# A streaming encoder step: stick-breaking probabilities kept in PSUM, two gates moved to the SSM, the sample normed into its own operand

## The chip, the cores and the metric

The kernel runs on one core of a Trainium2 chip. The metric is device time in microseconds for one launch, the median of three runs.

## What is computed

One layer of a hybrid encoder over 1024 prompt tokens and, with the same weights, 64 sample tokens that also see 2048 cached keys and values. A normed input is projected to q, k, v (8 heads of 64), to the SSM's input u and to two sets of gates. Attention is stick-breaking, and an S5 state-space branch runs beside it; a gated merge, an output product, a SwiGLU feed-forward part and a gated embedding follow.

```python
def _sb_block(qb, start, k, v, q_offset):
    z = jnp.einsum('bqhd,bkhd->bhqk', qb, k) * (SB_HEAD_DIM ** -0.5)
    ...
    log_keep = jnp.where(visible, jax.nn.log_sigmoid(-z), 0.0)
    after = lax.cumsum(log_keep, axis=3, reverse=True) - log_keep
    w = jnp.where(visible, jnp.exp(jax.nn.log_sigmoid(z) + after), 0.0)
    return jnp.einsum('bhqk,bkhd->bqhd', w, v)
...
    merged = (jax.nn.sigmoid(g_attn) * (o_attn @ W['w_branch_attn'])
              + jax.nn.sigmoid(g_ssm) * (o_ssm @ W['w_branch_ssm']))
    x = x + _rmsnorm(merged @ W['w_out'], W['norm_mix_post'])
```

The kernel computes a row of w as sigmoid(z) times the product of sigmoid(-z) over all later keys: a multiplying scan from the right.

## The kernel before, in words

Products of fp32 precision are made of three passes (`mm3_iter`, lines 137 to 139) over a high and a low half of each operand; the halves of a weight unit are made by ScalarE (`wh`) and VectorE (`wl`) in `unit`. A projection unit of 128 output columns (`fm_iter`) is 8 steps x 3 passes x 3 chunks of tokens = 72 products. A **gate** is one such unit with a sigmoid behind it, stored to DRAM (`gates`, `columns`); there are 16. Two are made at the start. The other 14, and three columns of q, k, v for the first pair of heads, are one generator in `body`, `rest`. `fill(n)` takes n steps of it: they are the **fills**, TensorE work that is due late and placed where other work waits.

`rest` is drawn in this order: `fill(3 * G1)` after the SSM's scan (a step is a chunk there), then `ssm_out`, `fill(3 * G2)`, `glu`, and then attention.

*SSM.* `ssm_scan` runs on VectorE over `hist`. `ssm_out` copies the final states to `fs`, exchanges the halves of `hist` through transfers (`exchange`), transposes `fs` on TensorE for the output and then, per group, multiplies `ut` by `toep` and `hist` by `cm` (lines 577, 578), takes the gelu and stores the result for `glu`, which reads it back as `y` and splits it into `ya`.

*Attention.* `attention` projects pair 0 of the heads, then runs through the string `ORDER`, made by `order()`: a digit is a step of that head (four steps of two query blocks each), `d` a step of the sample's attention (five for each pair), `p` a third of a chunk of the next pair's projection, `g` a fill of the same size, `E` the early load of the merge's operands. `gs` says how many `g` fall into each pair of heads. The Tile framework then sets every engine's order from these; engines are in order and wait on semaphores.

A **stick** (`stick`) is one run of up to 512 keys for 128 queries: TensorE writes z to a PSUM bank of tag `z` (three banks); ScalarE makes p = sigmoid(-z) and w = sigmoid(z), both in SBUF; VectorE scans p in place from the right (line 735); GpSimd (for the first query block of a step, and for the sample) or VectorE (for the second) multiplies w by p shifted by one (line 737). Where a run continues one to its right, the last column is multiplied by the carried product on its own (line 739), and the new carried product is copied to a tile `cy` (line 742). Then w is transposed on TensorE into a `tr` bank (two banks), split into `wth` by ScalarE and `wtl` by VectorE, and multiplied by v into `av`. There are 116 sticks, 48 with a carried product.

`tok_out` transposes k and v of a pair for the outputs through tiles `ob`, two buffers.

*After attention.* `merge` makes the merged operand: prompt columns in `H`, the sample's in `HS` as high and low half. `mix_out` takes the sample first, then the prompt tiles, and writes the normed result with `pre` into `H`; `ffn_in` first copies the sample's part of `H` to `HD` (line 1214) and uses it in `decode_rows` (line 1182).

Of the kernel before, what the change touches and what calls it, by code (L numbers as in the profile page):

```python
# [8 lines left out]
F32 = mybir.dt.float32  # L9
# [8 lines left out]
SEQ = 1024  # L18
# [13 lines left out]
G1, G2 = 5, 4  # L32
# [33 lines left out]
ORDER = order(L=1.7, steps=(0, 0.23, 0.42, 0.76), d0=-0.09, d1=1.77, p0=-0.36, p1=1.49, gs=(9, 15, 3, 21), e=7)  # L66


class Net:
# [478 lines left out]
    def ssm_out(self, Q, U):  # L548
        nc = self.nc
        V, hist = nc.vector, self.hist  # L550

        ps = self.ps.tile([128, 512], F32, name="tr", tag="tr")
# [6 lines left out]
        for i in range(4):  # L559
            nc.tensor.transpose(ps[:16, i * 128:(i + 1) * 128], fs[:, i], self.ident)  # L560
        V.tensor_copy(fin, ps[:16].rearrange("g (i s) -> g i s", i=4))
        for i, o in enumerate((4, 5, 8, 9)):
            nc.sync.dma_start(self.O[o][0, 0].rearrange("(h g) p -> g h p", h=2),
                              fin[:, i].rearrange("g (h p) -> g h p", h=2))
# [3 lines left out]
        for b in range(2):  # L568
# [12 lines left out]
            for t in range(T):  # L581
                for h in range(2):
                    nc.sync.dma_start(dst[b, t, :, h], src[t * 16:(t + 1) * 16, h, b])

# [143 lines left out]
    def stick(self, P, z, n, carry, more, e):  # L728

        nc = self.nc  # L730
        w = P.tile([128, 512], F32, "w", "w")[:, :n]
        p = P.tile([128, 512], F32, "p", "p")[:, :n]
        nc.scalar.activation(p, z, AF.Sigmoid, scale=-1.0)  # L733
        nc.scalar.activation(w, z, AF.Sigmoid)
        nc.vector.tensor_tensor_scan(p[:, ::-1], p[:, ::-1], self.zero.to_broadcast([128, n]),  # L735
                                     1.0 if carry is None else carry, op0=OP.mult, op1=OP.add)
        (nc.gpsimd if e == 'g' else nc.vector).tensor_tensor(w[:, :n - 1], w[:, :n - 1], p[:, 1:], op=OP.mult)  # L737
        if carry is not None:
            nc.vector.tensor_tensor(w[:, n - 1:], w[:, n - 1:], carry, op=OP.mult)  # L739
        if more:  # L740
            carry = P.tile([128, 1], F32, "cy", "cy")
            nc.vector.tensor_copy(carry, p[:, 0:1])
        return w, carry
# [322 lines left out]
    def mix_out(self, P, U):  # L1066
# [5 lines left out]
        for t in (8, 0, 4, 1, 5, 2, 6, 3, 7):  # L1072
# [20 lines left out]
            self.pre(P, x, gp, *(self.H[:, :, i, c0:c0 + r] for i in range(2)), hook=hooks.get(t))  # L1093
# [115 lines left out]
    def ffn_in(self, PT, P):  # L1209
# [3 lines left out]
        HD = P.pool.tile([128, 8, 2 * DEC], F32R, name="HD")  # L1213
        A.activation(HD.rearrange("p k (i t) -> p k i t", i=2), self.H[:, :, :, SEQ:], AF.Copy)
# [262 lines left out]
def body(tc, I, O, dbg=None, upto=99):  # L1477
    with ExitStack() as ctx:
# [69 lines left out]
        PAA = pools(tc, "attA", dict(hl=2, qb0=1, qs0=2, raw=1, vs0=2, vn0=1, ob=2, kn0=1))  # L1548
        with pools(tc, "att", dict(qs1=2, vs1=2, vn1=1, kn1=1, qb1=1, ks=3, w=6, p=3, cy=6, wth=2, wtl=2,
                                   ot=1, o=1, od=1, kr=1, vc=1, kk=1, wtd=1), "right") as P:  # L1550
            N.ps.alias = {}
            N.attention(P, PAA, fill, early)
            with N.hold(1):
                fill(48)
# [6 lines left out]
        N.ps.alias = MAL  # L1561
        with pool("wout", "right") as PW:
            N.HS = PW.tile([128, 8, 2 * DEC], F32R, name="HS")
# [8 lines left out]
        with pool("tok", "right") as PT, pools(tc, "ffn1", dict(raw=2, dh=1, dl=1, st=3, s=4, g11=1, g12=1, g21=1, g22=1, u11=1, u21=1,  # L1572
                                                                  u22=1, q=1, y0=1, y1=1, yo=1)) as P:
            N.ps.alias = WAL
            N.ffn_in(PT, P)
        PA = ctx.enter_context(pools(tc, "acc", dict(ss=4, xr=1, xn=2, hT0=1, hT1=1)))
# [35 lines left out]
```

## Time and profile before

| | |
|---|---|
| median of three runs | 1753.33 us (1753.03 to 1759.03) |
| the profiled execution's own time | 1759.74 us |
| its span | 1758.0 us |
| TensorE (PE) busy | 1693.2 us, 96% |
| VectorE (DVE) busy | 1036.4 us, 59% |
| ScalarE (ACT) busy | 729.7 us, 42% |
| GpSimd (POOL) busy | 520.9 us, 30% |
| mean granted TensorE clock | 0.984 |

The profile is that of one execution. Busy times of an engine are unions of its instructions' spans; products on TensorE are pipelined, so the duration of one is about twice the distance at which they follow each other. An idle time is put down to the instruction whose end released the engine. [...]

### The profile page before, as it was taken

To read this page: it belongs to the slowest core of one execution; us is meant where nothing else is said; L and a number is where in the kernel's file an instruction comes from. 1 tells how busy PE (TensorE), PEld (TensorE's weight loads), DVE (VectorE), ACT (ScalarE), POOL (GpSimd) and SP (SyncE) were. 2 spreads that over 40 slices of the span, in tenths; PEclk is the share of its full clock that TensorE was granted. 3 is DMA by queue.
4 is the path that set the end of the run, shared out by engine and by line. 5 is a ranking of instruction groups with operands and counts; after the bars stand their busy time and mean duration, and the time that the engine had idled before them with its cause. 6 is when DMAs were issued, how large, how long until landed. Compare 5 with 4: busy or idle time off the path is not lost.

```text
span 1758.0 us, 24713 instructions
## 1 busy us (share of the span) xinstructions
PE 1693.2 (96%) x9092; PEld 1479.8 (84%) x9092; DVE 1036.4 (59%) x1579; ACT 729.7 (42%) x1355; POOL 520.9 (30%) x450
## 2 busy tenths in 40 slices
PE   8999999999999898899999999999999999999998
PEld 6999998988898877798787888888888877888886
DVE  7437916337777767767464655555555456445674
ACT  6431135125555555633344433333333344444542
POOL 2026200012323223224231544445444212001453
PEclk9999999999999989999999999999999999999999
DMA  8362563884444343147445544446444386655332
GB/s 286 92 153 64 126 137 110 249 213 102 105 102 107 70 109 89 56 151 236 144 157 184 164 140 139 146 133 199 140 140 148 109 302 206 205 189 169 106 110 89
DMA packets 220713, 258.23 MB, mean 147 GB/s; under 512 B 26144, under 2 KB 168592, under 8 KB 220576
## 3 DMA queue, kind: packets, MB, share of 16 engines
q1 hardware_dynamic: 219936, 255.20, 48.0%
q0 software_dynamic: 656, 1.44, 0.6%
q8 instruction: 72, 1.18, 0.3%
q14 instruction: 49, 0.40, 0.1%
HBM read 165.32 MB, written 76.51 MB: 138 GB/s over the span
## 4 chain that ended last, share of the span: by engine, by line
PE 75%; DVE 12%; DMA 5%; ACT 3%; issue 3%; POOL 1%; SPq 1%; DVEq 0%; POOLq 0%; ACTq 0%
PE pj L1206 14%; PE tr L1206 8%; PE pj L137 6%; PE pj L139 6%; PE pj L138 6%; PE z L1372 3%; PE z L1206 3%; DVE p L735 3%; PE pj L1372 3%; PE tr L1372 2%; PE av L811 2%; PE z L138 2%; PE z L139 2%; PE z L137 2%; PE tr L781 1%
## 5 line engine op out<-in xcount | busy, mean ns | idle before, releaser
L137 PE MATMUL pj<-H,wh 128*128 128x362 f32 (+3 forms) x648 | 218.4, 337 | 5.9 <-DVE ql L634 3.6
L139 PE MATMUL pj<-H,wl 128*128 128x362 f32 (+3 forms) x648 | 215.8, 334 | 0.6 <-DVE wl L115 0.6
L138 PE MATMUL pj<-H,wh 128*128 128x362 f32 (+3 forms) x648 | 215.4, 333 | 0.0
L126 DVE TENSOR_TENSOR wl<-raw,wh 128x1024 fp32r<-128x1024 f32 x96 | 136.2, 1422 | 113.0 <-ACT wh L125 109.8
L737 POOL TENSOR_TENSOR w<-w,p 128x383 f32<-128x383 f32 (+4 forms) x68 | 92.7, 1373 | 315.2 <-DVE w L739 187.6
L125 ACT ACTIVATE wh<-raw 128x1024 fp32r<-128x1024 f32 x96 | 101.1, 1058 | 112.7 <-PE z L1372 44.4
L137 PEld LDWEIGHTS pj<-H,wh 128*128 128x128 f32 x648 | 123.3, 190 | 7.6 <-DVE ql L634 3.9
L139 PEld LDWEIGHTS pj<-H,wl 128*128 128x128 f32 x648 | 123.1, 190 | 1.5 <-DVE wl L115 1.0
L138 PEld LDWEIGHTS pj<-H,wh 128*128 128x128 f32 x648 | 123.3, 190 | 0.9 <-issue 0.4
L1206 PE MATMUL pj<-H,s 128*128 128x512 f32 x480 | 118.2, 395 | 0.0
L148 POOL TENSOR_TENSOR rs<-rs,mhalf 128x1 f32<-128x1 f32 (+1 forms) x54 | 32.6, 606 | 279.2 <-DVE rs L147 279.1
L1206 PEld LDWEIGHTS pj<-H,s 128*128 128x128 f32 x480 | 89.9, 188 | 20.9 <-DVE c L1239 0.3
L125 ACT ACTIVATE s<-st 128x512 fp32r<-128x512 f32 x80 | 50.3, 629 | 127.6 <-PE pj L1206 116.8
L1140 POOL TENSOR_TENSOR st<-raw 128x512 f32<-128x512 f32 x40 | 61.3, 1532 | 126.4 <-issue 52.3
L126 DVE TENSOR_TENSOR s<-st,s 128x512 fp32r<-128x512 f32 x80 | 64.4, 805 | 41.5 <-ACT s L125 40.9
L119 ACT ACTIVATE wh<-raw 128x1024 fp32r<-128x1024 f32 (+1 forms) x52 | 46.6, 898 | 98.9 <-PE av L138 51.4
L115 DVE TENSOR_TENSOR wl<-raw,wh 128x1024 fp32r<-128x1024 f32 (+1 forms) x50 | 51.0, 1021 | 57.9 <-ACT wh L119 57.8
L785 ACT ACTIVATE wth<-tr 128x512 fp32r<-128x512 f32 (+2 forms) x112 | 50.3, 453 | 83.3 <-PE tr L781 42.8
L786 DVE TENSOR_TENSOR wtl<-tr,wth 128x512 fp32r<-128x512 f32 (+2 forms) x112 | 55.2, 496 | 49.4 <-ACT wth L785 48.9
L733 ACT ACTIVATE p<-z 128x512 f32<-128x512 f32 (+4 forms) x116 | 59.0, 509 | 42.6 <-PE z L835 16.7
L735 DVE TENSOR_TENSOR_SCAN p<-p,zero 128x384 f32<-128x384 f32 (+4 forms) x68 | 73.9, 1094 | 0.2
L1206 PE MATMUL pj<-H,wh 128*128 128x512 f32 x224 | 71.1, 394 | 0.6 <-ACT H L125 0.4
(553 smaller groups left out, 4626.8 us busy)
## 6 DMA issues: line engine op xcount, KB each, us to landing
sd<-c SPq DMA_DIRECT2D x77, 256.0 KB, 3.1
raw<-sd SPq DMA_DIRECT2D x77, 256.0 KB, 2.8
raw<-in_w_in_dram SPq DMA_DIRECT2D x32, 512.0 KB, 5.4
raw<-in_w_ffn_gate_dram SPq DMA_DIRECT2D x22, 512.0 KB, 3.7
raw<-in_w_ffn_up_dram SPq DMA_DIRECT2D x22, 512.0 KB, 4.8
wd<-in_w_ffn_down_dram SPq DMA_DIRECT2D x44, 256.0 KB, 3.4
td<-wd SPq DMA_DIRECT2D x22, 512.0 KB, 3.1
raw<-td SPq DMA_DIRECT2D x44, 256.0 KB, 3.0
```

The costliest lines, as they stand in the source:

```text
L125: self.nc.scalar.activation(wh, raw, AF.Copy)
L126: self.nc.vector.tensor_sub(wl, raw, wh)
L137: self.nc.tensor.matmul(out, wh, xh, start=i == 0, stop=False)
L138: self.nc.tensor.matmul(out, wh, xl, start=False, stop=False)
L139: self.nc.tensor.matmul(out, wl, xh, start=False, stop=i == n - 1)
L733: nc.scalar.activation(p, z, AF.Sigmoid, scale=-1.0)
L735: nc.vector.tensor_tensor_scan(p[:, ::-1], p[:, ::-1], self.zero.to_broadcast([128, n]), 1.0 if carry is None else carry, op0=OP.mult, op1 ...
L737: (nc.gpsimd if e == 'g' else nc.vector).tensor_tensor(w[:, :n - 1], w[:, :n - 1], p[:, 1:], op=OP.mult)
L786: nc.vector.tensor_sub(wl[:, a:b], ps[:, a:b], wh[:, a:b])
L1140: op(t, x, y)
L1206: self.nc.tensor.matmul(out, a[i][:, k], b[j][:, k], start=start and k == i == j == 0, stop=stop and k == 3 and i == 1, skip_group_check=n ...
L1372: nc.tensor.matmul(B[b + n], x[:, 0, c], y[:, 1], start=new and p == j == 0, stop=p == 10 and j == 2, skip_group_check=not new)
```

## The change

- `stick`: w is made first; sigmoid(-z) is written over z in its PSUM bank; the scan reads that bank and writes p, now a tile of 513 columns whose last column holds the carried product. One product then covers the carried column too. The carried product is copied into column 512 of the tile that the next run will use (`late`). Lines 739 and the tile `cy` are gone.
- `G1` 5 to 6, `G2` 4 to 5, `gs` (9, 15, 3, 21) to (9, 12, 3, 6): a gate more ahead of the SSM's output, one more behind it, 18 steps of `g` (two gates) fewer in attention.
- `ssm_out`: the states' transposes and their stores come behind the output products, in a `z` bank instead of a `tr` bank.
- `mix_out`, `ffn_in`: the sample is normed into `HS`, which lives on until the feed-forward part; the tile `HD` and its copy are gone.
- Buffers: `w` 6 to 5, `p` 3 to 5 (wider), `cy` gone, `ob` 2 to 1.

```diff
-G1, G2 = 5, 4
+G1, G2 = 6, 5
...
-ORDER = order(L=1.7, steps=(0, 0.23, 0.42, 0.76), d0=-0.09, d1=1.77, p0=-0.36, p1=1.49, gs=(9, 15, 3, 21), e=7)
+ORDER = order(L=1.7, steps=(0, 0.23, 0.42, 0.76), d0=-0.09, d1=1.77, p0=-0.36, p1=1.49, gs=(9, 12, 3, 6), e=7)
...
     def ssm_out(self, Q, U):
-        ps = self.ps.tile([128, 512], F32, name="tr", tag="tr")
         fin = Q.tile([16, 4, 128], F32, name="fin")
         fs = Q.tile([128, 4, 16], F32, name="fs")
...
         self.exchange(hist[:, :, :, :NCH], X)
-        for i in range(4):
-            nc.tensor.transpose(ps[:16, i * 128:(i + 1) * 128], fs[:, i], self.ident)
-        V.tensor_copy(fin, ps[:16].rearrange("g (i s) -> g i s", i=4))
-        for i, o in enumerate((4, 5, 8, 9)):
-            nc.sync.dma_start(self.O[o][0, 0].rearrange("(h g) p -> g h p", h=2),
-                              fin[:, i].rearrange("g (h p) -> g h p", h=2))
...
+        ps = self.ps.tile([128, 512], F32, name="z", tag="z")
+        for i in range(4):
+            nc.tensor.transpose(ps[:16, i * 128:(i + 1) * 128], fs[:, i], self.ident)
+        V.tensor_copy(fin, ps[:16].rearrange("g (i s) -> g i s", i=4))
...
-    def stick(self, P, z, n, carry, more, e):
+    def stick(self, P, z, n, late, more, e):
         w = P.tile([128, 512], F32, "w", "w")[:, :n]
-        p = P.tile([128, 512], F32, "p", "p")[:, :n]
-        nc.scalar.activation(p, z, AF.Sigmoid, scale=-1.0)
+        p = P.tile([128, 513], F32, "p", "p") if late is None else late
+        c = 512 - n
         nc.scalar.activation(w, z, AF.Sigmoid)
-        nc.vector.tensor_tensor_scan(p[:, ::-1], p[:, ::-1], self.zero.to_broadcast([128, n]),
-                                     1.0 if carry is None else carry, op0=OP.mult, op1=OP.add)
-        (nc.gpsimd if e == 'g' else nc.vector).tensor_tensor(w[:, :n - 1], w[:, :n - 1], p[:, 1:], op=OP.mult)
-        if carry is not None:
-            nc.vector.tensor_tensor(w[:, n - 1:], w[:, n - 1:], carry, op=OP.mult)
+        nc.scalar.activation(z, z, AF.Sigmoid, scale=-1.0)
+        nc.vector.tensor_tensor_scan(p[:, c:512][:, ::-1], z[:, ::-1], self.zero.to_broadcast([128, n]),
+                                     1.0 if late is None else p[:, 512:], op0=OP.mult, op1=OP.add)
+        m = n - (late is None)
+        (nc.gpsimd if e == 'g' else nc.vector).tensor_tensor(w[:, :m], w[:, :m], p[:, c + 1:c + 1 + m], op=OP.mult)
         if more:
-            carry = P.tile([128, 1], F32, "cy", "cy")
-            nc.vector.tensor_copy(carry, p[:, 0:1])
-        return w, carry
+            late = P.tile([128, 513], F32, "p", "p")
+            nc.vector.tensor_copy(late[:, 512:], p[:, c:c + 1])
+        return w, late
...
-            self.pre(P, x, gp, *(self.H[:, :, i, c0:c0 + r] for i in range(2)), hook=hooks.get(t))
+            out = (self.H[:, :, i, c0:c0 + r] for i in range(2)) if t < 8 else (self.HS[:, :, i * DEC:i * DEC + DEC] for i in range(2))
+            self.pre(P, x, gp, *out, hook=hooks.get(t))
...
-        HD = P.pool.tile([128, 8, 2 * DEC], F32R, name="HD")
-        A.activation(HD.rearrange("p k (i t) -> p k i t", i=2), self.H[:, :, :, SEQ:], AF.Copy)
+        HD = self.HS
...
-        PAA = pools(tc, "attA", dict(hl=2, qb0=1, qs0=2, raw=1, vs0=2, vn0=1, ob=2, kn0=1))
-        with pools(tc, "att", dict(qs1=2, vs1=2, vn1=1, kn1=1, qb1=1, ks=3, w=6, p=3, cy=6, wth=2, wtl=2,
+        PAA = pools(tc, "attA", dict(hl=2, qb0=1, qs0=2, raw=1, vs0=2, vn0=1, ob=1, kn0=1))
+        with pools(tc, "att", dict(qs1=2, vs1=2, vn1=1, kn1=1, qb1=1, ks=3, w=5, p=5, wth=2, wtl=2,
```

How the change moves instructions, as built. TensorE in the SSM, before: the second pair of the states' transposes stands amid the fills that run ahead of the first `z<-hist` (`av<-H` are products of a gate, `fs` the copied states).

```order
L139 MATMUL av<-H,wl 128x362
L137 MATMUL av<-H,wh 128x362
L138 MATMUL av<-H,wh 128x362
L560 MATMUL tr<-ident,fs 16x128 x2
L139 MATMUL av<-H,wl 128x362
L137 MATMUL av<-H,wh 128x362
L138 MATMUL av<-H,wh 128x362
```

The same engine now: all four stand amid the fills behind the last `z<-hist`.

```order
L139 MATMUL pj<-H,wl 128x362
L137 MATMUL av<-H,wh 128x362
L138 MATMUL av<-H,wh 128x362
L579 MATMUL z<-ident,fs 16x128 x4
L139 MATMUL av<-H,wl 128x362
L137 MATMUL av<-H,wh 128x362
L138 MATMUL av<-H,wh 128x362
```

From row 929, where a gate begins in both, to the first `z<-hist` there are 172 rows before and 171 now: 169 and 170 products of gates. Behind the last `z<-hist` 93 stood before the first product of `glu`; now it is 245.

VectorE in attention, the start of a step of the sample and the heads beside it, before (the scan is listed as SCALAR_TENSOR_TENSOR, of line 735; `ba` is the merge's early operand):

```order
L735 SCALAR_TENSOR_TENSOR p<-p,cy,zero 128x512
L739 TENSOR_TENSOR w<-w,cy 128x1
L735 SCALAR_TENSOR_TENSOR p<-p,zero 128x384
L742 COPY cy<-p 128x1
L735 SCALAR_TENSOR_TENSOR p<-p,zero 128x512
L742 COPY cy<-p 128x1
L798 TENSOR_TENSOR o<-av,ot 64x256
L737 TENSOR_TENSOR w<-w,p 128x511
```

And now, the same place (the scan is line 737, the product line 740, the copy line 743):

```order
L737 SCALAR_TENSOR_TENSOR p<-z,p,zero 128x512
L743 COPY p<-p 128x1
L737 SCALAR_TENSOR_TENSOR p<-z,zero 128x384
L743 COPY p<-p 128x1
L737 SCALAR_TENSOR_TENSOR p<-z,zero 128x512
L799 TENSOR_TENSOR o<-av,ot 64x256
L740 TENSOR_TENSOR w<-w,p 128x511
L743 COPY p<-p 128x1
```

The order of the steps stayed; the single-column products went out and the scans read z.

Fills between one product `z<-kk,qb` or `z<-kn,qb` and the next, in TensorE's order, for the twenty steps of the sample (the last counted to the merge):

| | |
|---|---|
| before | 119, 34, 96, 51, 12, 75, 72, 111, 57, 21, 57, 57, 72, 30, 24, 0, 33, 57, 30, 120 |
| now | 135, 18, 96, 51, 12, 75, 63, 105, 48, 21, 57, 57, 81, 21, 9, 0, 9, 15, 9, 102 |

## Rows read from the trace of the kernel before

**Rows 1.** The page, part 1: engine, busy us, share of the span, instructions.
```profile
PE 1693.2 (96%) x9092; PEld 1479.8 (84%) x9092; DVE 1036.4 (59%) x1579; ACT 729.7 (42%) x1355; POOL 520.9 (30%) x450
```

**Rows 2.** Timeline of PE: start us, us, engine line operation [idle before, releaser].
```profile
197.45 0.39 PE L560 MATMUL tr<-ident,fs 128*16 128x128 f32 x2 [1.52 <-DVE fs L555]
...
222.34 0.60 PE L560 MATMUL tr<-ident,fs 128*16 128x128 f32 x2 [3.18 <-DVE fs L556]
...
232.49 0.39 PE L578 MATMUL z<-hist,cm 128*128 128x137 f32 x2
...
250.80 0.28 PE L578 MATMUL z<-hist,cm 128*128 128x137 f32 x1
...
268.89 0.49 PE L137 MATMUL tr<-ya,wh 128*128 128x364 f32 x1 [2.38 <-ACT ya L125]
...
344.71 0.33 PE L139 MATMUL tr<-bs,wl 128*128 128x362 f32 x1
345.21 0.33 PE L139 MATMUL tr<-bs,wl 128*128 128x362 f32 x1
```

**Rows 3.** Windows: stretch, busy us (x) of PE, PEld, DVE, ACT, POOL, granted clock.
```profile
220.00:230.00 10.00, 7.66 (x32) 7.59 (x32) 5.08 (x24) 1.06 (x1) 0.00 (x0) 0.66 0.53 138
```

**Rows 4.** Windows of three seven-scan cycles of attention, columns as before.
```profile
431.10:453.50 22.40, 20.86 (x134) 18.04 (x132) 18.24 (x28) 13.28 (x28) 6.34 (x4) 1.00 0.41 97
671.80:695.30 23.50, 18.94 (x116) 16.33 (x115) 18.36 (x31) 13.20 (x29) 6.33 (x4) 0.93 0.25 72
695.30:714.70 19.40, 18.81 (x123) 17.16 (x124) 16.38 (x30) 13.14 (x30) 5.37 (x4) 1.00 0.35 111
```

**Rows 5.** Timeline of DVE, SP and ACT around the end of the SSM scan.
```profile
208.81 1.22 DVE L115 TENSOR_TENSOR wl<-raw,wh 128x1024 fp32r<-128x1024 f32 x1
...
224.98 0.63 SPq L543 DMA_DIRECT2D us<-hist  x1
...
230.12 1.11 ACT L545 COPY hist<-us 64x1096 f32<-64x1096 f32 x1 [0.70 <-DMA us<-hist]
```

**Rows 6.** Groups by line and form: count, busy us, mean ns, idle before.
```profile
L735 DVE TENSOR_TENSOR_SCAN p<-p,zero 128x512 f32<-128x512 f32 x24 | 40.6, 1691 | 0.1
L739 DVE TENSOR_TENSOR w<-w,cy 128x1 f32<-128x1 f32 x48 | 12.8, 267 | 0.0
L737 DVE TENSOR_TENSOR w<-w,p 128x511 f32<-128x511 f32 x32 | 28.2, 881 | 1.5
L737 POOL TENSOR_TENSOR w<-w,p 128x511 f32<-128x511 f32 x24 | 43.9, 1828 | 201.8 <-DVE w L739 170.5 <-PE pj L139 13.7 <-ACT p L733 12.1
L733 ACT ACTIVATE p<-z 128x512 f32<-128x512 f32 x56 | 34.2, 610 | 29.6 <-PE z L835 16.7 <-POOL w L737 6.3 <-PE av L811 4.1
```

**Rows 7.** Timeline of DVE, POOL and PE in the cycles before 696 and at 754.
```profile
665.84 0.69 DVE L786 TENSOR_TENSOR wtl<-tr,wth 128x512 fp32r<-128x512 f32 x1 [1.25 <-ACT wth L785]
...
666.24 1.60 POOL L715 TENSOR_TENSOR vs<-ob,vs 128x256 fp32r<-128x256 f32 x2
...
673.63 1.28 DVE L735 TENSOR_TENSOR_SCAN p<-p,cy,zero 128x512 f32<-128x512 f32 x1 [1.27 <-ACT p L733]
...
675.02 0.95 DVE L735 TENSOR_TENSOR_SCAN p<-p,zero 128x384 f32<-128x384 f32 x1
...
676.07 1.86 DVE L735 TENSOR_TENSOR_SCAN p<-p,zero 128x512 f32<-128x512 f32 x1
...
677.85 0.63 PE L764 MATMUL z<-ks,qs 128*128 128x512 f32 x2
...
682.92 0.67 DVE L737 TENSOR_TENSOR w<-w,p 128x511 f32<-128x511 f32 x1
...
753.70 1.09 POOL L737 TENSOR_TENSOR w<-w,p 128x511 f32<-128x511 f32 x1 [3.58 <-DVE w L739]
```

**Rows 8.** DMA issues, 360 to 700 us: count, KB each, median us to landing.
```profile
out_dram<-ob SPq DMA_DIRECT2D x15, 256.0 KB, 2.4
```

**Rows 9.** Waits of PE, 930 to 950 us: us, times, longest.
```profile
PE z L1182 <- ACT HD L1214: 1.7, 1, 1.7
```

More of the change, by code (lines that the diff above doesn't have):

```diff
@@ L583, in ssm_out @@
                     nc.sync.dma_start(dst[b, t, :, h], src[t * 16:(t + 1) * 16, h, b])
+        ps = self.ps.tile([128, 512], F32, name="z", tag="z")
+        for i in range(4):
+            nc.tensor.transpose(ps[:16, i * 128:(i + 1) * 128], fs[:, i], self.ident)
+        V.tensor_copy(fin, ps[:16].rearrange("g (i s) -> g i s", i=4))
+        for i, o in enumerate((4, 5, 8, 9)):
+            nc.sync.dma_start(self.O[o][0, 0].rearrange("(h g) p -> g h p", h=2),
+                              fin[:, i].rearrange("g (h p) -> g h p", h=2))
     def glu(self, P):
@@ L1561, in body @@
         N.ps.alias = MAL
+        hs = pool("hs", "right")
+        N.HS = hs.__enter__().tile([128, 8, 2 * DEC], F32R, name="HS")
         with pool("wout", "right") as PW:
-            N.HS = PW.tile([128, 8, 2 * DEC], F32R, name="HS")
             with pools(tc, "mrgB", dict(braw=1, ga=2, gs=2)) as P:
@@ L1575, in body @@
             N.ffn_in(PT, P)
+        hs.__exit__(None, None, None)
         PA = ctx.enter_context(pools(tc, "acc", dict(ss=4, xr=1, xn=2, hT0=1, hT1=1)))
```

## The prediction

> **What bounds the kernel now.** I read the page first: TensorE is busy 1693.2 us, 96% of the span of 1758.0 [rows 1], so all that any edit can win beside removed TensorE work is 65 us of idle time, and what a lowered clock costs. The profiled execution took 1759.74 us, 6.4 above the median of the runs, 1753.33; differences below are taken from the first and applied to the second. Next I asked the waits and the timeline of TensorE where it stands still. Two places concern the change.
>
> First, the SSM. Fills are issued about 0.167 us apart (the last two rows of [rows 2]: three products in 0.50 us). Amid them TensorE stands 1.52 and 3.18 us for the two transposes of `fs`, and 2.38 us at the first GLU product [rows 2]. [...]
>
> Second, attention. I cut it at the products `z<-kk,qb` of `decode`, one per step of the sample, into 20 cycles, and asked for busy times by cycle. Twelve cycles have seven scans. In eight of these the fill is 57 products or fewer and VectorE has 16 to 18.5 us to do: they start at 431.1, 531.5, 578.5, 628.0, 671.8, 695.3, 714.7 and 738.5 and last 179.5 us together [rows 4]. Here the number of fills hardly sets the length: by the built order the cycle at 671.8 has 33 and takes 23.5 us, the one at 431.1 has 51 and takes 22.4 [rows 4]. VectorE, and the chain through ScalarE, GpSimd and the two `tr` banks, sets it. In the other cycles TensorE is busy nearly throughout, and a fill costs its 0.167 us.
>
> **The change, part by part.**
>
> *Two gates into the SSM: +18.7 us there.* A gate is 72 products, two are 144, or 24.0 us at 0.167. How much falls into gaps? By the built order the first `z<-hist` still has 170 fills ahead of it after 195.9 us (169 now), but no `fs` transposes. So TensorE comes earlier, and what is late next is `hist`: the exchange's transfers are issued at 224.98 when the scan ends, and its copy on ScalarE is done at 230.12 + 1.11 = 231.2 [rows 5]. VectorE's order in the scan is the same, so the second unit's low half is still ready at 208.81 + 1.22 = 210.0 [rows 5], where TensorE, no longer held, would arrive at 208.3. From 210.0 the remaining 98 fills last until 226.4: it idles 4.8 us for `hist`. Then come 17.2 us in place of 18.5 (from 232.5 to 251.0 [rows 2]), with 18 fills in between where 26 were, and some 2.5 us for the lowered clock, from the stretch that fell to 0.66 [rows 3]: until 250.9. Then 245 fills and the four transposes, 41.5 us, which cover the GLU's wait for `ya` completely, then 432 GLU products at 0.166: 364.2 us. Now the last of them ends at 345.5 [rows 2]. So 24.0 us of work cost 18.7; the gap moves more than it closes. The bounds are 15 (`hist` and the second unit in time) and 24 (nothing covered).
>
> *Fill taken from attention: -6.5 us.* Counting fills between two `z<-kk,qb` in both orders, the 144 come off as follows: 105 in the eight VectorE-bound cycles (9, 9, 24, 42 and 21 in the second, fourth, fifth, sixth and seventh of them), which I price at nothing because VectorE's time covers them, and a net 39 where TensorE is the bound (+16, -16, -9, -6, +9, -15 and, behind the last scan, -18): 39 x 0.167 = 6.5. Were none covered it would be 24.0; that is the far bound.
>
> *The scan reads PSUM; the carried column goes: -16.8 us.* Per seven-scan cycle: three single-column products at 0.267 are gone, 0.8 [rows 6]. The scans of 512 with a constant start average 1.69 us [rows 6], but 1.28 is what a 512 scan takes with GpSimd quiet, against 1.86 while GpSimd multiplies [rows 7]. A VectorE product with one input in PSUM kept its 0.69 us beside GpSimd at work [rows 7]. I therefore take the scans at the quiet price: 24 x 0.41 plus a little for the others, 12 us over 116 scans, 0.7 to 0.9 a cycle. VectorE's own 511 product is lifted from 0.67 to a mean of 0.88 by the same collisions [rows 6, 7]; two a cycle, 0.4. A weight split now and then moves out with the gates, 0.3. GpSimd's product, 1.83 on average and 1.09 where nothing met it [rows 6, 7], ends earlier and releases transposes, 0.3 more. Against it: the scan now follows ScalarE's second sigmoid, not its first, and at the start of a cycle VectorE has nothing else: +0.61 [rows 6]. Net 2.1 us in eight cycles, 16.8. Bounds: nothing, if PSUM is no quieter and the later start costs its 0.6 four times a cycle; 27 if the shorter chain counts in all twelve long cycles (2.25 each).
>
> What a scan from PSUM costs by itself no row shows. VectorE's 512 difference from PSUM takes no longer than the 0.67 to 0.69 of one from SBUF [rows 7], so I add nothing; the bounds are 0 and the 0.41 that would undo the quiet price. [...]
>
> *One `ob` buffer instead of two: +2 us.* The second and third copies of K's transposes now wait for the transfer before them, 2.4 us to landing [rows 8], with VectorE's queue (`wtl` for the next products) behind them. Twice in each of three pairs would be 14 us of VectorE waiting. But in two of the three the built order has 18 or more fills on TensorE around them, 3 us each, so I take 2. Bounds 0 and 14.
>
> *The sample normed into `HS`: -1.7 us.* The copy to `HD` goes, and with it the 1.7 us for which TensorE waits for it [rows 9]. Nothing covers it now and nothing replaces it, as `HS` is complete long before. Removed SBUF pressure elsewhere (`w` 5 for 6, `p` 5 for 3) I cost at nothing: five tiles are one cycle's.
>
> **Sum:** 18.7 - 6.5 - 16.8 + 2 - 1.7 = -4.3 us: 1755.4 for the profiled execution, **1749** on the median. Half a per cent, 8.8 us, is about what a measurement of this kernel can tell from no change, so I forecast no change that can be told.
>
> **Rivals.**
> *A, the attention gains more.* All twelve long cycles shorten, by 2.25 us, `ob` costs nothing, and the second unit's low half is no obstacle (-1.7): 17.0 - 6.5 - 27 - 1.7 = -18, 1735. For it: GpSimd's products shrink from 1.83 towards 1.09 in every cycle, and the transposes and `wtl` follow them. Against it: the four cycles with over 57 fills have TensorE busy nearly all the time. Part of it, about 1740, is the more probable form.
>
> *B, slower: PSUM banks come free too late.* Three `z` banks serve the queue. Now a bank is free after the second sigmoid; then only after its scan, on VectorE, behind whatever stands there. In a long cycle four of seven `z` must wait for a scan three places back. A new `z` needs about 0.63 us on TensorE [rows 7], two sigmoids at 0.61 [rows 6] and some 0.15 of signalling: 2.0 us, while two scans, 0.95 for 384 and 1.28 for 512, last 2.2 [rows 7]. It decides against the change as soon as that chain grows by 0.3 us: then VectorE waits, TensorE stands in its order with transposes behind it. Two such waits of 0.7 us in twelve cycles are 17 us: 1766. For it: the fills that filled those waits are just the ones removed. Against it: in the built order `z` is spread between transposes. [...] No row here shows yet what holding a bank costs.
>
> *C, the scans stay as slow.* Should GpSimd hold VectorE up as before, only the removed columns (0.8) and the moved splits count, less the later start: 0.5 x 8 = 4, and the sum is +8.5, 1762. [...]
>
> **How the numbers follow.** Forecast 0.52, its own range 1742 to 1757; of it 0.13 falls below 1744.5 and 0.02 above 1762. A 0.25, nearly all faster (0.23). B 0.15, slower but for 0.02. C 0.08, on the border: 0.06 same, 0.02 slower. Faster 0.13 + 0.23 = 0.36; same 0.37 + 0.02 + 0.02 + 0.06 = 0.47; slower 0.02 + 0.13 + 0.02 = 0.17. The range for 8 in 10 runs from A's end to the middle of B: 1735 to 1763.
>
> **What would show it.** Right: TensorE waits near 226 us for `hist` and nowhere before the GLU, whose last product ends near 364; scans of 512 read 1.2 to 1.3 us in every place and GpSimd's 511 product close to 1.1; the eight long cycles fall by some 2 us each though their fill is gone; attention ends about 20 us after that with 144 fills fewer; no wait at the first L1182. Wrong: scans above 1.5 us (C); TensorE standing at `z<-ks,qs` until a scan (B); cycles shortened by the fills they lost (then VectorE was not the bound, and A or more holds).

## The result and the profile after

| | before | after |
|---|---|---|
| median | 1756.70 us (6 runs, 1753.03 to 1759.03) | 1770.26 us (6 runs, 1766.91 to 1772.89) |
| profiled execution, its own time | 1759.74 us | 1769.70 us |
| its span | 1758.0 us | 1767.6 us |

The ratio is 1.0079, with a 95% interval of 1.0064 to 1.0093: slower by 0.8%, outside the range of the prediction, which had seen no change as the likeliest. By the medians that is 13.6 us; the two profiled executions lie 10.0 us apart. The page of the changed kernel, part 1, answers to [rows 1]:

```profile
PE 1693.1 (96%) x9092; PEld 1473.7 (83%) x9092; DVE 1005.4 (57%) x1531; ACT 733.4 (41%) x1354; POOL 485.8 (27%) x450
```

TensorE is busy as long as before, VectorE 31 us and GpSimd 35 us less. So the 9.6 us by which the span grew are idle time on TensorE: 1767.6 - 1693.1 = 74.5 us against 1758.0 - 1693.2 = 64.8.

**The SSM went as forecast.** TensorE's timeline of the changed kernel, start and duration in us, answers to [rows 2]:

```profile
229.77 0.80 PE L570 MATMUL z<-hist,cm 128*128 128x137 f32 x2 [4.66 <-DVE hist L546]
...
249.74 0.40 PE L570 MATMUL z<-hist,cm 128*128 128x137 f32 x2
...
290.89 0.33 PE L137 MATMUL pj<-ya,wh 128*128 128x364 f32 x1
...
362.43 0.33 PE L139 MATMUL pj<-bs,wl 128*128 128x362 f32 x1
```

One wait of 4.66 us for `hist`, none for `ya`, and the GLU's last product ends at 362.8 instead of 345.5: 17.2 us later, for 24 us of work moved there.

**The scans became short too.** Groups by form in attention, changed kernel, columns as in [rows 6]:

```profile
L737 DVE TENSOR_TENSOR_SCAN p<-z,p,zero 128x512 f32<-128x512 f32 x32 | 40.5, 1275 | 28.4 <-ACT z L736 28.4
...
L740 POOL TENSOR_TENSOR w<-w,p 128x512 f32<-128x512 f32 x24 | 30.0, 1251 | 209.2 <-DVE p L737 209.2
L737 DVE TENSOR_TENSOR_SCAN p<-z,zero 128x512 f32<-128x512 f32 x24 | 29.3, 1220 | 2.5 <-ACT z L736 2.5
...
L740 DVE TENSOR_TENSOR w<-w,p 128x511 f32<-128x511 f32 x24 | 16.3, 679 | 0.1
```

1.22 us for 1.69, GpSimd's product 1.25 for 1.83, VectorE's 0.68 for 0.88 [rows 6].

**But attention gave back too little.** From the GLU's last product to the merge's first it lasts 413.1 us, 13.0 less than before, where the prediction's terms made 21.3. What VectorE waited for before its copies to `ob`, from 365 to 775 us, first in the kernel before and then in the changed one:

```profile
its engine sat idle before it (us, times) until:
  PE tr L705: 7.8, 7
  DMA out_dram<-ob: 3.6, 2
```

```profile
its engine sat idle before it (us, times) until:
  DMA out_dram<-ob: 19.9, 7
```

**And the merge grew by 5.2 us**, from 48.2 to 53.4 between its first and its last product. Two waits in TensorE's timeline there that the kernel before does not have, and ScalarE's timeline ahead of the first:

```profile
789.14 0.43 PE L137 MATMUL z<-ba,wh 128*128 128x364 f32 x1 [1.10 <-ACT wh L119]
...
821.86 0.43 PE L139 MATMUL pj<-ba,wl 128*128 128x364 f32 x1 [1.99 <-DVE wl L115]
```

```profile
785.84 0.51 ACT L125 ACTIVATE H<-ga 128x362 fp32r<-128x362 f32 x1 [0.80 <-POOL ga L946]
788.06 0.51 ACT L125 ACTIVATE H<-ga 128x364 fp32r<-128x364 f32 x1 [1.71 <-POOL ga L946]
788.47 1.14 ACT L119 ACTIVATE wh<-raw 128x512 fp32r<-128x512 f32 x2
```

The split of the next weights stands behind pieces of `H<-ga` that wait for GpSimd. In the kernel before it stands ahead of them:

```profile
780.99 0.63 ACT L119 ACTIVATE wh<-raw 128x512 fp32r<-128x512 f32 x1 [1.64 <-PE av L138]
781.53 0.49 ACT L125 ACTIVATE H<-ga 128x364 fp32r<-128x364 f32 x1
```

### The profile page after: what moved, and what is told of

Same layout as the page of the kernel before. It is cut to its first block, busy times and chain, and to the rows that moved or that the text cites. A ratio compares the mean times of both kernels' runs of the same rounds, so it can differ in the third digit from the quotient of the medians.

```text
span 1767.6 us, 24576 instructions
## 1 busy us (share of the span) xinstructions
PE 1693.1 (96%) x9092; PEld 1473.7 (83%) x9092; DVE 1005.4 (57%) x1531; ACT 733.4 (41%) x1354; POOL 485.8 (27%) x450
## 3 DMA queue, kind: packets, MB, share of 16 engines
q8 instruction: 71, 1.16, 0.3%
## 4 chain that ended last, share of the span: by engine, by line
PE 76%; DVE 11%; DMA 7%; ACT 3%; issue 2%; POOL 1%; SPq 1%; DVEq 0%; POOLq 0%; ACTq 0%
PE pj L1208 14%; PE tr L1208 7%; PE pj L137 7%; PE pj L139 6%; PE pj L138 6%; PE z L1373 3%; PE z L1208 3%; PE pj L1373 3%; DVE p L737 2%; PE z L138 2%; PE z L137 2%; PE z L139 2%; PE tr L1373 2%; PE av L1373 1%; PE z L765 1%
## 5 line engine op out<-in xcount | busy, mean ns | idle before, releaser
L137 PE MATMUL pj<-H,wh 128*128 128x362 f32 (+3 forms) x632 | 211.6, 335 | 5.5 <-DVE ql L634 2.8
L139 PE MATMUL pj<-H,wl 128*128 128x362 f32 (+3 forms) x632 | 209.0, 331 | 0.4 <-DVE wl L115 0.4
L138 PE MATMUL pj<-H,wh 128*128 128x362 f32 (+3 forms) x632 | 208.9, 331 | 0.0
L740 POOL TENSOR_TENSOR w<-w,p 128x383 f32<-128x383 f32 (+4 forms) x68 | 61.5, 908 | 328.4 <-DVE p L737 327.8
L137 PEld LDWEIGHTS pj<-H,wh 128*128 128x128 f32 x632 | 119.5, 189 | 7.7 <-DVE ql L634 2.9
L138 PEld LDWEIGHTS pj<-H,wh 128*128 128x128 f32 x632 | 119.1, 189 | 0.8 <-issue 0.4
L139 PEld LDWEIGHTS pj<-H,wl 128*128 128x128 f32 x632 | 119.0, 188 | 0.8 <-DVE wl L115 0.6
L1208 PEld LDWEIGHTS pj<-H,s 128*128 128x128 f32 x480 | 89.8, 188 | 20.9 <-DVE c L1240 0.3
L787 DVE TENSOR_TENSOR wtl<-tr,wth 128x128 fp32r<-128x128 f32 (+2 forms) x112 | 54.4, 494 | 47.1 <-ACT wth L786 46.7
L786 ACT ACTIVATE wth<-tr 128x128 fp32r<-128x128 f32 (+2 forms) x112 | 49.3, 448 | 69.7 <-PE tr L782 55.0
L735 ACT ACTIVATE w<-z 128x512 f32<-128x512 f32 (+4 forms) x116 | 57.8, 498 | 37.2 <-PE z L836 15.9
L737 DVE TENSOR_TENSOR_SCAN p<-z,p,zero 128x512 f32<-128x512 f32 (+1 forms) x48 | 52.0, 1094 | 28.4 <-ACT z L736 28.4
```

The costliest lines, as they stand in the source:

```text
L137: self.nc.tensor.matmul(out, wh, xh, start=i == 0, stop=False)
L138: self.nc.tensor.matmul(out, wh, xl, start=False, stop=False)
L139: self.nc.tensor.matmul(out, wl, xh, start=False, stop=i == n - 1)
L737: nc.vector.tensor_tensor_scan(p[:, c:512][:, ::-1], z[:, ::-1], self.zero.to_broadcast([128, n]), 1.0 if late is None else p[:, 512:], op ...
L740: (nc.gpsimd if e == 'g' else nc.vector).tensor_tensor(w[:, :m], w[:, :m], p[:, c + 1:c + 1 + m], op=OP.mult)
L787: nc.vector.tensor_sub(wl[:, a:b], ps[:, a:b], wh[:, a:b])
```

## The experiments

The stages of each profiled execution, from TensorE's timeline, in us: the end of the GLU's last product, from there to the first product of the merge (attention), and from that to the merge's last. "Profiled" is that execution's own time. Executions of one kernel scatter by some 4 us about their median, and the profiled ones lie on either side of it (e17's is 7 us above), so a single profile tells stages apart, and the medians tell the sum. Each run was measured beside runs of the kernel before, whose median was 1754.7 to 1756.8; "over before" is the difference from those, and the ratio is to them as well. Where two runs were not measured together, their difference is better read from this column than from the medians.

| run | GLU ends | attention | merge | profiled | median | over before | ratio to before, 95% |
|---|---|---|---|---|---|---|---|
| before | 345.5 | 426.1 | 48.2 | 1759.7 | 1756.7 | | |
| after | 362.8 | 413.1 | 53.4 | 1769.7 | 1770.3 | +13.6 | 1.0064 to 1.0093 |
| e1_old_fill | 344.6 | 424.8 | 53.5 | 1761.7 | 1763.7 | +8.4 | 1.0029 to 1.0063 |
| e2_gates_only | 360.8 | 420.8 | 48.7 | 1770.1 | 1773.5 | +18.2 | 1.0085 to 1.0121 |
| e3_ob2 | 363.0 | 409.3 | 53.4 | 1768.9 | 1764.6 | +9.3 | 1.0031 to 1.0068 |
| e4_HD_copy | 363.6 | 412.1 | 53.0 | 1767.7 | 1771.4 | +16.1 | 1.0067 to 1.0110 |
| e5_scan_sbuf | 362.2 | 431.7 | 53.9 | 1792.0 | 1786.4 | +29.6 | 1.0147 to 1.0190 |
| e6_scan_psum_only | 363.0 | 405.2 | 48.1 | 1760.9 | 1758.2 | +1.4 | 0.9988 to 1.0012 |
| e7_psum_old_fill | 343.9 | 418.7 | 48.1 | 1752.4 | 1753.0 | -3.8 | 0.9972 to 0.9992 |
| e8_column_old_fill | 344.5 | 426.6 | 48.1 | 1759.2 | 1762.9 | +6.1 | 1.0023 to 1.0046 |
| e9_merge_order | 364.2 | 418.6 | 48.1 | 1773.8 | 1773.5 | +18.5 | 1.0093 to 1.0122 |
| e10_ob1 | 364.2 | 408.0 | 48.1 | 1762.6 | 1766.3 | +11.2 | 1.0050 to 1.0076 |
| e11_pool_products | 346.7 | 412.2 | 48.3 | 1750.1 | 1750.1 | -4.9 | 0.9967 to 0.9989 |
| e12_psum_alone | 343.3 | 417.1 | 48.6 | 1749.2 | 1751.1 | -3.9 | 0.9971 to 0.9991 |
| e13_column_psum | 342.6 | 413.8 | 53.5 | 1748.8 | 1751.3 | -3.4 | 0.9974 to 0.9991 |
| e14_w4_p5 | 362.3 | 403.1 | 52.7 | 1757.7 | 1756.4 | +1.7 | 0.9990 to 1.0013 |
| e15_psum_pool | 342.7 | 413.8 | 48.1 | 1743.2 | 1743.2 | -11.5 | 0.9920 to 0.9957 |
| e16_psum_pool_hs | 345.7 | 411.9 | 48.1 | 1749.0 | 1748.0 | -6.7 | 0.9946 to 0.9975 |
| e17_column_pool | 343.3 | 415.1 | 54.2 | 1756.1 | 1749.1 | -6.4 | 0.9954 to 0.9977 |
| e18_w4_ob1 | 363.2 | 410.8 | 53.2 | 1767.2 | 1767.2 | +11.7 | 1.0052 to 1.0078 |

The first theory was that the gates cost and the scans pay; its rival, that the gates are neutral and the scans (with a z bank held until its scan) lose.

**e1_old_fill**, the changed kernel:

```diff
-G1, G2 = 6, 5
+G1, G2 = 5, 4
-ORDER = order(L=1.7, steps=(0, 0.23, 0.42, 0.76), d0=-0.09, d1=1.77, p0=-0.36, p1=1.49, gs=(9, 12, 3, 6), e=7)
+ORDER = order(L=1.7, steps=(0, 0.23, 0.42, 0.76), d0=-0.09, d1=1.77, p0=-0.36, p1=1.49, gs=(9, 15, 3, 21), e=7)
```


> The changed kernel with the gates and the attention's fill where they were before (5 and 4 gates, 9, 15, 3 and 21 steps of fill), everything else as changed. Theory 1 (the two gates are what costs: 17.2 us more in the SSM and the GLU, of which attention returns only a part, while the scans from PSUM do help): the first GLU products end near 345 us again, attention is shorter than before by some 5 to 12 us at equal fill, and the time is 1745 to 1752, below the kernel before. Theory 2 (the gates are neutral, 17 us spent and about as much returned, and the scans from PSUM, with a z bank held until its scan and one ob buffer, are what loses): 1760 to 1770, above the kernel before.

**e2_gates_only**: the same two lines the other way round, in the kernel before.

> The kernel before with only the fill moved (6 and 5 gates into the SSM, 9, 12, 3 and 6 steps in attention), scans, buffers and HD as they were. Theory 1: 18 us more in the SSM and GLU, of which attention returns 6 to 10, since its long cycles are set by VectorE with or without the fill: 1764 to 1769. Theory 2: attention returns nearly all of the 24 us of work: 1752 to 1759, no slower than the kernel before.

Neither theory holds for both runs. Undoing the gates leaves the kernel 8 us slower than before, as the second theory said, so something besides them loses. The gates alone cost 18 us, above even the first theory's range, so they are not neutral either. Attention returned 5.3 us in the profile of e2, for 15.3 us more ahead of it; the profile of e2 is of its shortest execution and that of the kernel before lies 3 us above its median, so these stages show less than the medians.

**e3_ob2**, the changed kernel with `ob=2` and `p=4` for 5.

> The changed kernel with two ob buffers again (and, to make room, four p buffers for five). If the single ob buffer costs little, as I had reckoned: 1767 to 1770, some 2 us less than the changed kernel's 1770. If it holds VectorE at each pair of heads: 1756 to 1760. If four p buffers bind: above 1772.

5.7 us less by the medians (4.3 over their own runs of before): between the first two cases, and a first sign of the single buffer.

**e4_HD_copy**, the changed kernel with the sample's norm into `H`, the tile `HD` with its copy, and `HS` in the pool `wout`, all three as before.

> The changed kernel with the sample's activations as before: normed into H, copied to HD by ScalarE, and HS inside the mixer's pool. If HS only saves the wait for that copy: 1772, 1.7 us more than the changed kernel. If the new place of HS is what makes the merge 5 us longer after the change (TensorE waits 1.1 and 2.0 us there for weight splits): 1766 to 1767, 3 to 4 us less, and the merge's last product comes 47.8 us after its first and not 53.1.

1771.4 and a merge of 53.0 us: the place of `HS` has nothing to do with the merge, and that guess fell.

**e5_scan_sbuf**, the changed kernel:

```diff
+        nc.scalar.activation(p[:, c:512], z, AF.Sigmoid, scale=-1.0)
         nc.scalar.activation(w, z, AF.Sigmoid)
-        nc.scalar.activation(z, z, AF.Sigmoid, scale=-1.0)
-        nc.vector.tensor_tensor_scan(p[:, c:512][:, ::-1], z[:, ::-1], self.zero.to_broadcast([128, n]),
+        nc.vector.tensor_tensor_scan(p[:, c:512][:, ::-1], p[:, c:512][:, ::-1], self.zero.to_broadcast([128, n]),
```


> The changed kernel with the scan back in SBUF: ScalarE writes the second sigmoid, first in order, into the probabilities' tile and the scan runs in place there; the carried column, the moved fill, one ob and HS stay. If the scan from PSUM relieves VectorE as the shorter scans of the changed kernel's trace say (31 us less VectorE time, 35 us less GpSimd time), attention gets longer by 5 to 12 us: 1775 to 1782. If the held z banks (20 us of waits behind scans would be the most, 6.4 are seen) give all of it back, it is the same within 4 us: 1766 to 1774.

16 us slower than the changed kernel, more than expected, and attention is 18.6 us longer. The scan's source is the part that pays. Its group in that run, both kinds of start together, and that of GpSimd's product, up to 775 us:

```profile
L736 DVE TENSOR_TENSOR_SCAN p<-p,zero 128x512 f32<-128x512 f32 x54 | 79.1, 1470 | 22.2 <-ACT p L734 21.8
L739 POOL TENSOR_TENSOR w<-w,p 128x512 f32<-128x512 f32 x23 | 39.5, 1716 | 203.6 <-DVE p L736 164.5 <-PE z L764 23.5 <-PE av L811 12.2
```

**e6_scan_psum_only**, the changed kernel, but with this scan, shown against the kernel before (the lines after it, the tile `cy` and the buffers `w=6, p=3, cy=6, ob=2` as before):

```diff
-        nc.scalar.activation(p, z, AF.Sigmoid, scale=-1.0)
         nc.scalar.activation(w, z, AF.Sigmoid)
-        nc.vector.tensor_tensor_scan(p[:, ::-1], p[:, ::-1], self.zero.to_broadcast([128, n]),
+        nc.scalar.activation(z, z, AF.Sigmoid, scale=-1.0)
+        nc.vector.tensor_tensor_scan(p[:, ::-1], z[:, ::-1], self.zero.to_broadcast([128, n]),
```


> The changed kernel with the scan from PSUM, but with the separate carried column, its single-column product and the buffers of before (six w, three p, two ob). In the built order the merge's loads and splits of weights then stand as in the kernel before. If the merge's 5 us come from that order and the single ob costs 3 to 4 us: 1761 to 1764. If the carried column in the tile is worth something (three products of 0.27 us in each cycle, 6 to 10 us in all): 1768 to 1774.

**e7_psum_old_fill**: the scan of e6 in the kernel before, with the new `ssm_out` and `HS`; gates, `gs` and buffers as before.

> The kernel before with three parts only: the scan from PSUM (separate carried column, buffers as before), the final states' transposes behind the exchange, and HS. Gates and fill as before. Theory: it leaves out what costs (gates, single ob, the merge's order) and keeps the relief, so 1748 to 1754, below the 1755 of the kernel before. Rival: with the old fill TensorE is the bound of most cycles and holding the z banks costs more than the scans save, as the first run with the old fill suggested: 1757 to 1764.

e6 is level with the kernel before, 12 us below the changed one and below both of its ranges; e7 is faster than both kernels, as its theory said. Between the two lie the gates alone: they cost 5.2 us with the scan from PSUM, where they had cost 18 without it. They pay in neither.

**e8_column_old_fill**: the scan of e5 (in SBUF, with the carried column in p) in the kernel before, with the new `ssm_out` and `HS`; `w=5, p=4, ob=2`.

> The kernel before with the carried column in the products' tile (five w, four p, two ob), the scan in SBUF as before, the transposes behind the exchange, and HS. Theory: single-column products gone, 0.8 us a cycle at most, of which little reaches the end: 1750 to 1755. Rival, the longer-lived tiles hold the chain up: above 1757.

The rival held: 6 us slower than before. The carried column without the scan from PSUM loses.

**e9_merge_order**, the changed kernel with `gs=(9, 12, 3, 4)`.

> The changed kernel with 4 steps of fill instead of 6 beside the last pair of heads (the two steps run after the last scan). In the built order the merge's weight loads and splits then stand as in the kernel before, with the load of the next weights ahead of the two gate loads. Theory: the merge's 5 us belong to that order, so its products take some 48.2 us from first to last (53.4 in the changed kernel) and the time is 1764 to 1767. Rival, that the merge is longer because attention's last heads deliver late: it stays at 53, and 1769 to 1772.

A miss. The merge takes 48.1 us, as the order said, but attention takes 418.6 us and the total is 3 us higher. The 18 fills that were beside the last heads now run behind the last scan, 3.0 us of work at 0.167, and the last stretch before the merge is 2.3 us longer; the first cycle is 3.1 us longer too, with the same 168 products, at a granted clock of 0.90 for 0.95 (1.00 is full speed). So the run shows that the merge's length follows the built order, and not that the total does.

**e10_ob1**: e6 with `ob=1`.

> The run with the scan from PSUM alone and the moved fill (six w, three p), with one ob buffer instead of two. If the single buffer is what costs 4 to 6 us (as two ob with four p suggested): 1762 to 1764.5 against the 1758 of that run. If four p for five had paid in that other run: 1757 to 1760.

8.1 us slower than e6 by the medians, 9.8 over their own runs of before, for a single buffer: past the expected end. VectorE's waits for `ob` in attention, in e6 and then in e10:

```profile
  DMA out_dram<-ob: 1.3, 2
```

```profile
  DMA out_dram<-ob: 17.8, 6
```

**e11_pool_products**: e7 with `EH = 'gg'` for `'gv'`, so that both products of a pair of scans are GpSimd's.

> The fastest kernel so far (scan from PSUM, separate column, fill as before) with both products of each pair of scans on GpSimd, where now one of them is VectorE's. GpSimd's time in attention fell from 113 to 77 us, so it has room. If VectorE's share of the chain is still the bound: some 29 us less VectorE work, 1 us off each of eight long cycles, 1744 to 1749. If the products' latency counts (1.2 us on GpSimd against 0.68 on VectorE, and two behind each other): 1757 to 1775, slower.

1750.1, a microsecond above the first case. Against e7 that is 2.9 us by the medians and 1.1 over their own runs of before, so a gain over e7 is not shown by this pair.

**e12_psum_alone**: the kernel before with the lines of e6 and nothing else.

> The kernel before with the scan from PSUM alone: neither the transposes nor HS are touched. If the scan makes up the gain of the fastest run: 1753 to 1756. HS should be worth the 1.7 us that TensorE waits for HD, the transposes' place 0.9: without them 2 to 3 us more than that run's 1753.

Below the expected range. It gains all that e7 gains (-3.9 and -3.8): HS and the transposes' place add nothing there.

What was priced so far, the scan (-3.9), the gates (+5.2) and one `ob` (+8.1), left some 4 us of the 13.6 to the carried column or its buffers.

**e13_column_psum**: the kernel before with the changed `stick` and `w=5, p=4`, `ob` 2 as before.

> The kernel before with the changed scan as a whole (from PSUM, carried column in the products' tile; five w, four p, two ob), fill, transposes and HS as before. If the column costs what it seemed to cost with the moved fill (6 us against the separate column): 1756 to 1758, where the scan from PSUM alone gave 1751. The merge then again takes 53 us from its first to its last product. If the column costs only where the fill is thin: 1750 to 1753.

The second case: level with e12. The merge is 53.5 us as expected, and attention 3.3 us shorter, so in the profiles the two nearly offset each other.

**e14_w4_p5**: the changed kernel with `ob=2, w=4`.

> The changed kernel with two ob and, to make room, four w (five p stay). If the count of four p was what held the run with two ob at 1764.6: 1758 to 1761. If neither count binds: 1763 to 1766. If w binds (two parts of a step hold four products at once): above 1768.

Below the first case: 14 us less than the changed kernel (11.9 over their own runs of before) and level with the kernel before.

**e15_psum_pool**: e12 with `EH = 'gg'`. **e16_psum_pool_hs**: that with `HS` as changed.

> The scan from PSUM alone with both products of a pair on GpSimd; nothing else changed. The same move gave 2.9 us (1753.0 to 1750.1) beside HS and the moved transposes. If it adds up: 1747 to 1749. If the two gains share the same slack: 1750 to 1752.

> The same with HS in place of the copy to HD. If TensorE's 1.7 us wait for HD is on the path: 1.7 less than without HS, 1745 to 1748. If the time for which it waits there is taken by the next wait: the same within 1 us.

e15, at 1743.2, is below both of its ranges, the fastest of all, and beats both kernels. e16 fits neither of its cases; it is 4.8 us slower than e15 and shows why `HS` gains nothing there. TensorE's waits at the start of the feed-forward part, in e15 and then in e16:

```profile
926.78 0.39 PE L1182 MATMUL z<-wh,HD 128*128 128x256 f32 x1 [1.68 <-ACT HD L1214]
...
930.34 0.50 PE L1206 MATMUL tr<-H,wl 128*128 128x512 f32 x1 [0.35 <-DVE wl L126]
```

```profile
927.92 0.74 PE L1207 MATMUL tr<-H,wh 128*128 128x512 f32 x2 [0.52 <-ACT wh L125]
929.10 0.70 PE L1207 MATMUL tr<-H,wh 128*128 128x512 f32 x2 [0.44 <-DVE t L1047]
931.47 0.80 PE L1207 MATMUL tr<-H,wl 128*128 128x512 f32 x1 [1.56 <-DVE wl L126]
```

The wait for the copy is replaced by waits for the weights' split, 2.52 us for 2.03. The larger part follows them: behind its wait at 931 us the granted clock is 0.50 and then 0.75 in e16, and stays at 1.00 in e15. Windows of both, columns as in [rows 3], first e15 and then e16 (the clock is the third number from the end):

```profile
930.00:934.00 4.00, 3.67 (x16) 3.01 (x17) 1.42 (x2) 1.02 (x2) 0.00 (x0) 1.00 0.83 186
934.00:939.00 5.00, 5.00 (x23) 4.07 (x22) 2.29 (x4) 2.60 (x5) 0.00 (x0) 1.00 1.02 372
```

```profile
931.00:935.00 4.00, 3.53 (x8) 2.81 (x9) 1.87 (x3) 0.59 (x2) 0.00 (x0) 0.50 0.68 159
935.00:940.00 5.00, 5.00 (x18) 3.99 (x17) 1.02 (x2) 1.51 (x3) 0.00 (x0) 0.75 0.98 340
```

In these nine microseconds e16 gets 26 products done and e15 39; at 0.23 us a product that is some 3 us. In the changed kernel's own trace the clock stays at 1.00 there, and e4, without `HS`, came out 1.1 us slower than it by the medians, within the scatter. So what `HS` is worth depends on the kernel around it, and in none of these runs is it shown to gain.

**e17_column_pool**: e15 with the changed `stick`, `w=4, p=5`. **e18_w4_ob1**: the changed kernel with `w=4`.

> The kernel before with the changed scan (from PSUM, carried column in the products' tile; four w, five p, two ob) and both products of a pair on GpSimd; fill, transposes and HS as before. Against the 1743.2 of the same without the column in the tile: 1740 to 1742.5 if the single-column products (48 of 0.23 us on VectorE) are on the path of the long cycles, 1743 to 1747 if they lie in VectorE's waits.

> The changed kernel with four w for five and nothing else: one ob, five p. If the 14 us between the changed kernel and the run with two ob and four w are the ob buffer's: 1768 to 1773, as the changed kernel. If the four w (another order of the planner) brought part of them: 1757 to 1766.

e17 missed on the high side. Its merge is 54.2 us, 6.1 longer than e15's, and its median is 6.0 higher; but its profile is 7 us above its median, so that the merge alone makes the difference is not shown. e18 falls just short of the first case: over their own runs of before, the count of `w` is worth 1.9 us (e18 for the changed kernel) and the `ob` buffer 10.0 (e14 for e18). VectorE waits 19.6 us for `ob` in e18 and 2.0 in e14.

## Why the prediction was wrong

By the differences over before, the way from the changed kernel (+13.6) back is: four `w` for five, -1.9 (e18); two `ob`, -10.0 (e14); the gates, the transposes and HS undone, with five `w` and four `p`, -5.1 (e13); the column, with its buffers, -0.5 (e12); the scan back in SBUF, +3.9 (before).

**The step that failed: "One `ob` buffer instead of two: +2 us".** Its price is 9.8 us (e10 against e6) to 10.0 (e18 against e14), good to some 3 us by the intervals. VectorE waited for `ob` 17.1 to 21.9 us in each of the seven runs with one buffer, and 1.3 to 3.6 in each of the thirteen with two. In the changed kernel it is 19.9 us, seven times, up to 4.1 at once; I had named 14 as the bound. I then took 2 because "in two of the three the built order has 18 or more fills on TensorE around them". All seven waits do lie in four cycles rich in fills (135, 96, 105 and 81 by the table of the built orders), and none in the eight cycles that VectorE was to set. The cover did not hold. One of the seven waits in the changed kernel, on VectorE and then on TensorE:

```profile
645.53 0.28 DVE L719 COPY ob<-tr 64x128 f32<-64x128 f32 x1 [3.65 <-DMA out_dram<-ob]
645.74 0.41 DVE L787 TENSOR_TENSOR wtl<-tr,wth 128x256 fp32r<-128x256 f32 x1
```

```profile
645.87 0.66 PE L830 MATMUL tr<-ident,kr 128*128 128x128 f32 x4 [1.56 <-DVE ob L719]
```

Behind the copy stand `wtl` in VectorE's queue and, on TensorE, the transposes of the cached keys `kr`, which need the `tr` bank that the copy empties; the next step's first `z` is made from them. TensorE reaches them 1.56 us before the copy lets it go on, and the products behind them wait as well. The cycle that holds this wait, in e14 with two buffers and in e18 with one:

```profile
613.60:637.50 23.90, 22.42 (x150) 20.55 (x148) 14.40 (x30) 11.59 (x29) 3.02 (x4) 1.00 0.49 120
```

```profile
617.20:646.00 28.80, 25.27 (x157) 23.31 (x156) 14.41 (x30) 11.89 (x30) 3.01 (x4) 0.94 0.47 110
```

It takes 23.8 to 24.3 us in all thirteen runs with two buffers and 25.6 to 28.8 in the seven with one. Part of that is fills: with one buffer the framework puts nine more into it (27 products of line 137 for 24) and some 16 more into the first of the four (45 for 40), so these shifts, which I entered under the fill, belong to the buffer as well. Over the whole of attention TensorE stands 4.1 us longer in e18 than in e14 and 5.4 longer in e10 than in e6; the rest of the 10 us is not located by single profiles.

**What that leaves.** From the forecast -4.3 to the measured +13.6 there are 17.9 us. The `ob` term has 8 of them, 10 for 2. The count of `w`, costed at nothing, has 1.9. The other 8.0 are seen in e14, which has two `ob` and four `w`: +1.7, where the sum without the `ob` term is -6.3. Of these 8 the profiles locate the merge (4.5 us longer in e14) and `HS`, below; the rest stays open.

**SSM +18.7**: right within 1.5, with the wait for `hist` (4.66 for 4.8) and the covered GLU. The 2.5 us for a lowered clock were an estimate, and such a stretch is there: behind that wait the granted clock is 0.50 from 229 to 235 us. In the kernel before it is 0.50 from 222.6 to 228.2 us, and the fills there follow each other 0.30 us apart, for 0.167.

**Fill -6.5 and scan -16.8**, together -23.3: right as a sum where the buffer does not disturb it. Attention is 20.9 us shorter than before in e6 and 23.0 in e14. The split between the two is not what I made it. The scan alone brings 9.0 (e12 in the profile), the gates alone bring 5.3 back (e2), and 14.3 is less than both together. By the differences over before the scan's source is worth 3.9 us alone (e12), 9.5 with the carried column and the old fill (e13 against e8) and 16 in the changed kernel (e5). The cycles show why. Seven of the eight that VectorE was to set (the eighth runs on to the merge) take 160.8 us before, 157.4 with the gates alone (e2), 152.8 with the scan alone (e12) and 145.9 with both (e6). So the 105 fills taken out of them, 17.5 us of work, gave 3.4 us with the slow scans and 6.9 with the fast ones: priced at nothing they were nearly right as long as VectorE was slow, and less so behind the very scans of this change.

**HS -1.7**: not seen. From the merge's last product to the end the changed kernel takes 938.3 us and the kernel before 938.2. In e16 the waits for the next split take the place of the one for the copy, and the granted clock behind them is 0.50 and 0.75, where e15 has 1.00.

**The merge** stood in no term, though its stage is the second largest part of the miss in the profiles. I compared the orders through attention only. There the framework had also put the merge's weight splits behind the gates' pieces, and its stage grew by 5.2 us. It does so in every run with the column and the scan from PSUM but e9, and in e5. Its length is shown to follow the order; what it is worth in the total isn't settled: 7.9 us (e3 against e6), 5.1 (e17 against e15), 0.5 (e13 against e12), all three with other counts of `w` and `p` as well.

**Rivals.** B, that z banks come free too late: the waits are there, 6.4 us in the changed kernel, and cost less than the scan gains:

```profile
PE z L765 <- DVE p L737: 6.4, 13, 1.1
```

It named the right sign, and a time (1766) 4 us from the measured one, for the wrong reason: that is luck. Its 0.15 us of signalling was an estimate; the trace of before shows 0.09 from the end of a `z` to its sigmoid (677.68 to 677.77) and 0.05 from ScalarE's `wth` to TensorE's product (665.81 to 665.86). Here a bank held about one scan longer was worth it, by the 3.9 us of e12. C, slow scans: excluded by 1.22 us, and by e5. With one input in PSUM the scan and GpSimd's product both shorten, 1.69 to 1.22 and 1.83 to 1.25, and in e5, with both inputs in SBUF, the product is back at 1.72 and the scans of both kinds at 1.47, where the changed kernel's average 1.25. Why the two engines' times move together no run shows. A, more gain: not seen. The 23.0 us of attention in e14 are the nearest to its 33.5 for scans and fill together, and e15 is fast by another edit.

## What to carry to other kernels

When a buffer count falls, price the wait on the engine that waits and on what stands behind it, in that engine's queue and in the buffers that it holds; work on another engine covers it only as long as that work lasts, and if the scheduler brought it there it is missing elsewhere. Compare the built orders to the end of the program, not only around the edit, since a scheduler moves what follows too. When an operand moves to PSUM, look at what the engine beside it gains: GpSimd, busy 36.6 us less in e12, had room for 48 more products, 32 of them of 511 columns, and that, beside the scan from PSUM and without the edit's other parts, made the fastest version (e15, 7.6 us below e12; beside HS and the moved transposes it brought 1.1, e11 against e7).

## What the runs showed that was not expected

A scan that reads PSUM was not seen to cost anything extra: with a carried start and 512 columns it takes 1.28 us, the same as one in SBUF with GpSimd quiet [rows 7].

GpSimd gains more from it than VectorE: in e12, with nothing else changed, 36.6 us of its time (520.9 to 484.3) against 21.9 (1036.4 to 1014.5). And its products stay short when it has 48 more of them, 1.16 us on average in e15:

```profile
L737 POOL TENSOR_TENSOR w<-w,p 128x511 f32<-128x511 f32 x56 | 64.7, 1155 | 179.7 <-DVE p L735 171.3 <-DVE w L739 8.3
```

The same 9092 products of TensorE keep it busy for 1687.1 us in e12 and 1683.2 in e15, against 1693.2 before:

```profile
PE 1687.1 (97%) x9092; PEld 1473.6 (84%) x9092; DVE 1014.5 (58%) x1579; ACT 732.0 (42%) x1355; POOL 484.3 (28%) x450
```

The mean granted clock of the timed executions was 0.987 for the kernel before (29 of them, run beside e5 to e8) and 0.990 for e7. So part of e7's 4 us may lie in the clock, which stood at 0.50 behind some of TensorE's stops (in the SSM of both kernels, and in e16); how much was not tried apart.
